# Batched product of x and y: loads of groups 4 to 11 issued from ScalarE's DMA queue instead of SyncE's, two steps later

## The chip, the cores and the metric

The kernel runs on one core of a Trainium2 chip. The metric is device time in microseconds (us), the median of 10 runs.

## The reference

For each of 96 pairs of batch and head (8 x 12), a 512 x 64 matrix x is multiplied by the transpose of a 512 x 64 matrix y. Inputs and output are float32.

```python
"x": np.random.randn(8, 12, 512, 64).astype(np.float32)
"y": np.random.randn(8, 12, 512, 64).astype(np.float32)
return np.einsum('bhtc,bhsc->bhts', x, y).astype(np.float32)
```

The inputs are 25.17 MB together, the output 100.66 MB. All of it crosses between HBM and SBUF once: 125.83 MB.

## The kernel before, in words

**Tiling.** The 96 heads are cut into 12 groups of 8 (`NG` = 12, `G` = 8). One group's x is one 1 MB load, xs, of 128 partitions with 8 KB each; its y is another, ys. A group gives four results of 2 MB (`half` 0 and 1, `h` 0 and 1), each gathered in one output tile `ot` of 128 partitions with 16 KB each and written by one store. So there are 24 loads and 48 stores.

**Stages of one group.** `casts` (L72) turns each half of xs and ys into bf16 in twelve instructions, which for groups 1 to 11 are all on GpSimd (L136). `transposes` (L100) makes xT and yT on VectorE with two 32 x 32 block transposes per half. `result` (L114) multiplies: for each k of 0, 2, 4, 6 two matmuls fill a PSUM tile `pm` of 128 x 1024, which is copied to `ot`, on ScalarE for k = 0, 2 and 6 (L128), on VectorE for k = 4 (L126). Then SyncE issues the store (L129).

**What sets the order.** The whole program stands under `manual_schedule`: each engine carries out its instructions in the order in which the Python code emits them. The main loop (L154) emits the four results of group g and, between their k steps, the preparation of group g + 1 as a generator, `prepare` (L131), of 16 steps; each k of each result takes one step. Steps 0 and 1 emit the casts, 5 and 13 the transposes, and step 12, which falls at k = 0 of the fourth result, emits the load of three groups further on (`AHEAD` = 3, L139). An engine that waits for a semaphore holds up everything behind it in its own order.

**The loads.** Groups 0, 1 and 2 are loaded at the start (L144) and group 3 after the casts of group 0 (L152). Groups 4 to 11 are loaded at step 12. All of them are issued on SyncE, as are the stores, so that loads and stores stand in one queue in the order of issue: from group 4 on two loads, then four stores, then two loads. A load waits until the casts have read the buffers that it overwrites.

**Buffers.** xs and ys have three buffers each, `ot` has seven, `pm` four. The framework also gives each DMA one of eight semaphores, in turn; a DMA whose semaphore still belongs to an unfinished one waits for that.

Of the kernel before, what the change touches and what calls it, by code (L numbers as in the profile page):

```python
# [1 line left out]

# [4 lines left out]


@with_exitstack
def kernel(  # L10
    ctx: ExitStack,
    tc: tile.TileContext,
    x: bass.AP,
    y: bass.AP,
    out: bass.AP,
):

    nc = tc.nc
    B, H, T, C = x.shape
    _, _, S, _ = y.shape
    P = 128
    G = 8
    Q = P // G  # L30
    R = T // Q
    NG = B * H // G
    K = 8
    E = R // K
    D = 32
    AHEAD = 3
    fp32 = mybir.dt.float32
    bf16 = mybir.dt.bfloat16
    u32 = mybir.dt.uint32
    COPY = mybir.ActivationFunctionType.Copy  # L40
    assert C == 2 * D and S == T and R == D and Q * 2 == D

    xv = x.rearrange("b h t c -> (b h t c)").rearrange("(g p n) -> g p n", p=P, n=R * C)
    yv = y.rearrange("b h t c -> (b h t c)").rearrange("(g p n) -> g p n", p=P, n=R * C)
    ov = out.rearrange("b h t s -> (b h t s)").rearrange(
        "(o u h q n) -> o h q u n", u=2, h=2, q=Q * E, n=K * S
    )

    const = ctx.enter_context(tc.tile_pool(name="const", bufs=1))
    lpool = ctx.enter_context(tc.tile_pool(name="lpool", bufs=AHEAD))  # L50
    ybpool = ctx.enter_context(tc.tile_pool(name="ybpool", bufs=2))
    tpool = ctx.enter_context(tc.tile_pool(name="tpool", bufs=4))
    opool = ctx.enter_context(tc.tile_pool(name="opool", bufs=7))
    pmpool = ctx.enter_context(tc.tile_pool(name="pmpsum", bufs=4, space=bass.MemoryType.PSUM))

    loaded, made = {}, {}
    zeroed = [const.tile([P, K * E * D], u32, name=f"xb{half}") for half in range(2)]

    def load(g):
        xs = lpool.tile([P, R, C], fp32)  # L60
        ys = lpool.tile([P, R, C], fp32)
        nc.sync.dma_start(xs.rearrange("p r c -> p (r c)"), xv[g])  # L62
        nc.sync.dma_start(ys.rearrange("p r c -> p (r c)"), yv[g])  # L63
        loaded[g] = (xs, ys)

    def cast(engine, dst, src):
        if engine is nc.scalar:
            nc.scalar.activation(dst, src, COPY)  # L68
        else:
            engine.tensor_copy(dst, src)  # L70

    def casts(g, half, engines):  # L72

        xs, ys = loaded[g]
        xb = zeroed[half]
        xv2 = xb.bitcast(bf16).rearrange("p (k e c u) -> p k e c u", k=K, e=E, u=2)
        base = half * 64
        n = 0
        for ch in range(2):
            for u in range(2):  # L80
                lo = base + u * D
                src = xs[lo:lo + D, :, ch * D:(ch + 1) * D]
                cast(
                    engines[n % len(engines)],
                    xv2[(2 * ch + u) * D:(2 * ch + u + 1) * D, :, :, :, u],
                    src.rearrange("p (e k) c -> p k e c", k=K),
                )
                n += 1
        yb = ybpool.tile([P, R // 2 * D], u32)
        yv2 = yb.bitcast(bf16).rearrange("p (j c w) -> p j w c", j=R // 2, w=2)  # L90
        for ch in range(2):
            cast(
                engines[n % len(engines)],
                yv2[ch * 64:(ch + 1) * 64],
                ys[base:base + 64, :, ch * D:(ch + 1) * D].rearrange("p (j w) c -> p j w c", w=2),
            )
            n += 1
        return xb, yb

    def transposes(g, half, xb, yb):  # L100
        xT = tpool.tile([P, K * D * E], u32)
        nc.vector.transpose(  # L102
            xT.rearrange("p (k r e) -> p k e r", k=K, e=E),
            xb.rearrange("p (k e c) -> p k e c", k=K, e=E),
        )
        yT = tpool.tile([P, D * R // 2], u32)
        nc.vector.transpose(  # L107
            yT.rearrange("p (r j) -> p j r", r=D), yb.rearrange("p (j c) -> p j c", c=D)
        )
        made[g, half] = (  # L110
            xT.bitcast(bf16).rearrange("p (k h m) -> p k h m", k=K, h=2), yT.bitcast(bf16)
        )

    def result(g, half, h, steps):  # L114

        xT, yT = made[g, half]
        ot = opool.tile([P, K, S], fp32)
        for k in range(0, K, 2):
            next(steps, None)
            pm = pmpool.tile([P, 2, S], fp32)  # L120
            for two in range(2):
                nc.tensor.matmul(  # L122
                    pm[:, two, :], xT[:, k + two, h, :], yT[:, h * S:(h + 1) * S], start=True, stop=True
                )
            if k == 4:
                nc.vector.tensor_copy(ot[:, k:k + 2, :], pm)  # L126
            else:
                nc.scalar.activation(ot[:, k:k + 2, :], pm, COPY)  # L128
        nc.sync.dma_start(ov[2 * g + half, h], ot.rearrange("p r s -> p (r s)"))  # L129

    def prepare(g):  # L131

        b = {}
        for step in range(16):
            if step in (0, 1):
                b[step] = casts(g, step, [nc.gpsimd])  # L136
            if step in (5, 13):
                transposes(g, step // 8, *b[step // 8])
            if step == 12 and g + AHEAD < NG:  # L139
                load(g + AHEAD)  # L140
            yield

    with tc.manual_schedule():
        for g in range(AHEAD):  # L144
            load(g)
        nc.vector.memset(zeroed[0], 0.0)  # L146
        nc.gpsimd.memset(zeroed[1], 0.0)  # L147
        b0 = casts(0, 0, [nc.vector, nc.scalar, nc.gpsimd])
        transposes(0, 0, *b0)
        b1 = casts(0, 1, [nc.gpsimd, nc.scalar])  # L150
        transposes(0, 1, *b1)
        if AHEAD < NG:  # L152
            load(AHEAD)
        for g in range(NG):  # L154
            steps = prepare(g + 1) if g + 1 < NG else iter(())
            for half in range(2):
                for h in range(2):
                    result(g, half, h, steps)
            for _ in steps:
                pass  # L160


# [1 line left out]
_INS = ['x', 'y']  # L164
_OUTS = [((8, 12, 512, 512), 'float32')]


# [23 lines left out]
```

## Time and profile before

| | |
|---|---|
| median of 10 runs | 304.45 us (303.43 to 305.06) |
| the profiled execution, its own time | 305.01 us |
| its span | 303.1 us |
| busy: PE, DVE, ACT, POOL | 45%, 43%, 48%, 60% |
| DMA queue of SyncE (q1) | 98.2% of 16 engines' span |
| load, from issue to landing | 26.2 us (xs), 26.5 us (ys), median of 12 each |
| store, from issue to landing | 32.8 us, median of 48 |

The busy shares are of the span of the profiled execution. POOL is GpSimd, DVE is VectorE, ACT is ScalarE, PE is TensorE, and SP is SyncE, which only issues. A share of the DMA queue is the time that its packets took, summed, over 16 times the span. The span lies 1.9 us below the execution's own time.

### The profile page before, as it was taken

The page shows a single profiled execution, that of the slowest core. Times are in us where ns is not written, and L with a number is a line of the kernel's source. Part 1 is how long each engine was busy: PE and PEld are TensorE (multiplying, and loading weights), DVE is VectorE, ACT ScalarE, POOL GpSimd, SP SyncE. Part 2 cuts the span into 40 slices and gives each one's busy share as a digit, 9 for nine tenths or more (in the row PEclk, how much of TensorE's full clock was granted, in tenths as well). Part 3 has the DMA queues.
Part 4 walks back from the last instruction along what each step waited for, and adds up shares of the span by engine and source line. Part 5 has one row for each costly group of instructions (what it writes and reads, how often), then busy time and mean ns, then how long its engine had stood idle before and what let it go on. Part 6 is the DMA issues. An engine that isn't in the chain of part 4 may idle for free.

```text
span 303.1 us, 1551 instructions
## 1 busy us (share of the span) xinstructions
PE 135.3 (45%) x384; PEld 46.5 (15%) x384; DVE 130.8 (43%) x99; ACT 145.0 (48%) x150; POOL 182.1 (60%) x142
## 2 busy tenths in 40 slices
PE   0567766654632554445184264444527556430000
PEld 0112222221210111111021021111102212100000
DVE  3856666666670651544247065154334661310000
ACT  2996656585561553364256064347334655650000
POOL 3899999999999985682772955668379100000000
PEclk9995767798995687598559567758955968975555
DMA  7999999999999999999999999999999999999992
GB/s 291 427 385 437 418 431 435 428 418 429 429 418 438 428 422 428 435 422 422 433 428 412 433 430 432 415 441 415 419 441 423 443 415 441 419 441 423 437 428 106
DMA packets 10377, 125.93 MB, mean 415 GB/s; under 512 B 1152, under 2 KB 1152, under 8 KB 1152
## 3 DMA queue, kind: packets, MB, share of 16 engines
q1 hardware_dynamic: 10368, 125.83, 98.2%
q8 instruction: 3, 0.05, 0.1%
q14 instruction: 6, 0.05, 0.0%
HBM read 25.17 MB, written 100.66 MB: 415 GB/s over the span
## 4 chain that ended last, share of the span: by engine, by line
DMA 75%; POOL 10%; ACT 2%; issue 1%; DVE 0%; ACTq 0%; PE 0%; SPq 0%; POOLq 0%
DMA out_dram<-ot 62%; DMA ys<-in_y_dram 12%; POOL xb L70 6%; POOL yb L70 3%; ACT ot L128 2%; DVE ot L126 0%; PE pm L122 0%; ACTq L186 0%; SPq L62 0%; POOLq L70 0%; ACTq L128 0%; SPq L129 0%; DVE yT L107 0%; SPq L63 0%
## 5 line engine op out<-in xcount | busy, mean ns | idle before, releaser
L128 ACT ACTIVATE ot<-pm 128x1024 f32<-128x1024 f32 x144 | 137.0, 1028 | 120.5 <-DMA out_dram<-ot 99.8
L122 PE MATMUL pm<-yT,xT 128*128 128x512 bf16 x384 | 135.3, 507 | 132.5 <-ACT ot L128 98.6
L70 POOL CAST xb<-xs 32x1024 bf16<-32x1024 f32 x91 | 120.4, 1323 | 50.0 <-DMA xs<-in_x_dram 32.1
L126 DVE COPY ot<-pm 128x1024 f32<-128x1024 f32 x48 | 58.1, 1215 | 114.8 <-DMA out_dram<-ot 108.6
L122 PEld LDWEIGHTS <-xT 128*128 128x128 bf16 x384 | 46.5, 121 | 220.5 <-issue 195.5
L70 POOL CAST yb<-ys 64x1024 bf16<-64x1024 f32 x46 | 60.5, 1316 | 3.3 <-DMA ys<-in_y_dram 0.6
L102 DVE STREAM_TRANSPOSE xT<-xb 128x1024 uint32<-128x1024 uint32 x24 | 49.3, 2053 | 13.3 <-POOL xb L70 11.9
L107 DVE STREAM_TRANSPOSE yT<-yb 128x512 uint32<-128x512 uint32 x24 | 24.9, 1038 | 6.2 <-POOL yb L70 6.2
L70 DVE CAST xb<-xs 32x1024 bf16<-32x1024 f32 x2 | 2.5, 1237 | 3.7 <-DMA xs<-in_x_dram 3.7
L68 ACT ACTIVATE xb<-xs 32x1024 bf16<-32x1024 f32 x3 | 4.0, 1345 | 0.1
L68 ACT ACT_TABLE_LOAD x1 | 1.3, 1283 | 5.6 <-DMA xs<-in_x_dram 5.6
L68 ACT ACTIVATE yb<-ys 64x1024 bf16<-64x1024 f32 x2 | 2.7, 1350 | 0.0
L146 DVE MEMSET xb<- 128x1024 uint32 x1 | 0.9, 912 | 1.0 <-PEq L175 1.0
L147 POOL MEMSET xb<- 128x1024 uint32 x1 | 1.0, 951 | 0.3 <-POOLq L175 0.3
L175 POOL MEMSET const-float32-0.0<- 128x1 f32 x1 | 0.1, 97 | 0.2 <-issue 0.2
L175 POOL MEMSET const-float32-1.0<- 128x1 f32 x1 | 0.1, 98 | 0.0
L175 POOL MEMSET const-bfloat16-1.0<- 128x1 bf16 x1 | 0.1, 98 | 0.0
L175 POOL MEMSET const-uint8-127<- 128x1 uint8 x1 | 0.1, 98 | 0.0
## 6 DMA issues: line engine op xcount, KB each, us to landing
out_dram<-ot SPq DMA_DIRECT2D x48, 2048.0 KB, 32.8
xs<-in_x_dram SPq DMA_DIRECT2D x12, 1024.0 KB, 26.2
ys<-in_y_dram SPq DMA_DIRECT2D x12, 1024.0 KB, 26.5
```

Source lines behind the costliest of these rows:

```text
L68: nc.scalar.activation(dst, src, COPY)
L70: engine.tensor_copy(dst, src)
L102: nc.vector.transpose(xT.rearrange("p (k r e) -> p k e r", k=K, e=E), xb.rearrange("p (k e c) -> p k e c", k=K, e=E),)
L107: nc.vector.transpose(yT.rearrange("p (r j) -> p j r", r=D), yb.rearrange("p (j c) -> p j c", c=D))
L122: nc.tensor.matmul(pm[:, two, :], xT[:, k + two, h, :], yT[:, h * S:(h + 1) * S], start=True, stop=True)
L126: nc.vector.tensor_copy(ot[:, k:k + 2, :], pm)
L128: nc.scalar.activation(ot[:, k:k + 2, :], pm, COPY)
L146: nc.vector.memset(zeroed[0], 0.0)
L147: nc.gpsimd.memset(zeroed[1], 0.0)
L175: nc = _bacc.Bacc("TRN2", target_bir_lowering=False, num_devices=1)
```

## The change

`load` gets the queue as an argument. The loads of groups 0 to 3 stay on SyncE. Those of groups 4 to 11 are emitted at step 14 in place of 12, and are issued by ScalarE. Step 14 falls at k = 4 of the fourth result. In ScalarE's order the two issues stand between the copies of k = 2 and of k = 6 of that result, and nothing else moves on ScalarE, VectorE, GpSimd or TensorE. SyncE is left with the first eight loads and then 48 stores in a row.

```diff
-    def load(g):
+    def load(g, queue):
...
-        nc.sync.dma_start(xs.rearrange("p r c -> p (r c)"), xv[g])
-        nc.sync.dma_start(ys.rearrange("p r c -> p (r c)"), yv[g])
+        queue.dma_start(xs.rearrange("p r c -> p (r c)"), xv[g])
+        queue.dma_start(ys.rearrange("p r c -> p (r c)"), yv[g])
...
-            if step == 12 and g + AHEAD < NG:
-                load(g + AHEAD)
+            if step == 14 and g + AHEAD < NG:
+                load(g + AHEAD, nc.scalar)
...
-            load(g)
+            load(g, nc.sync)
...
-            load(AHEAD)
+            load(AHEAD, nc.sync)
```

## Prediction

> **What bounds the kernel now.** I read the slices of the page first, then its queues, its chain and its DMA issues.
>
> ```profile
> DMA  7999999999999999999999999999999999999992
> GB/s 291 427 385 437 418 431 435 428 418 429 429 418 438 428 422 428 435 422 422 433 428 412 433 430 432 415 441 415 419 441 423 443 415 441 419 441 423 437 428 106
> DMA packets 10377, 125.93 MB, mean 415 GB/s; under 512 B 1152, under 2 KB 1152, under 8 KB 1152
> ...
> q1 hardware_dynamic: 10368, 125.83, 98.2%
> ...
> DMA 75%; POOL 10%; ACT 2%; issue 1%; DVE 0%; ACTq 0%; PE 0%; SPq 0%; POOLq 0%
> ...
> out_dram<-ot SPq DMA_DIRECT2D x48, 2048.0 KB, 32.8
> xs<-in_x_dram SPq DMA_DIRECT2D x12, 1024.0 KB, 26.2
> ```
>
> From the second slice to the last but one the 16 DMA engines are never short of work, and the chain is 75% DMA. A store lands 32.8 us after its issue, although 2.10 MB take only 4.9 us at 430 GB/s: some six transfers are queued ahead of it. The waits say the same from the other side: the evicting engines wait for output buffers to be written out.
>
> ```profile
> DVE ot L126 <- DMA out_dram<-ot: 108.6, 31, 9.5
> ACT ot L128 <- DMA out_dram<-ot: 99.8, 33, 7.9
> ...
> POOL xb L70 <- DMA xs<-in_x_dram: 32.1, 6, 6.3
> ```
>
> So the time is what the DMA engines need for 125.83 MB, and any microsecond that they gain or lose counts in full. How much is lost already? Stretches with and without loads, from the table of windows (last two columns: DMA share, GB/s):
>
> ```profile
> 94.00:143.00 49.00, 22.69 (x64) 7.72 (x64) 21.12 (x16) 22.84 (x24) 34.82 (x27) 0.72 1.01 428
> 143.00:192.00 49.00, 22.53 (x61) 7.49 (x61) 21.15 (x16) 22.75 (x24) 30.41 (x25) 0.66 1.01 426
> 192.00:219.00 27.00, 12.52 (x37) 4.26 (x36) 10.51 (x8) 11.52 (x13) 17.32 (x14) 0.79 1.00 425
> 225.00:290.00 65.00, 26.26 (x72) 8.70 (x71) 20.31 (x16) 28.13 (x30) 8.24 (x7) 0.68 1.01 431
> ```
>
> Stores alone (the last row) run at 431, loads and stores mixed at 425 to 428. A group moves 10.49 MB, which is 24.33 us at 431 and 24.56 at 427: about 0.2 us lost per group.
>
> The trace's packet records say where. The 72 transfers have 144 packets each: 128 with data and 16 of 4 bytes that close them, so each engine gets 8 data packets of each transfer. A store packet (16 KB) is recorded with 611 ns, a load packet (8 KB) with 309; on one engine the next starts some 4 ns before the last ends, so their pitch is 607 and 306 ns. Only one place is regularly longer: the last load packet of a pair of loads, the one with a store behind it. Over the eight later pairs the excess per engine is 0.08, 0.15, 0.11, 0.12, 0.24, 0.28, 0.15 and 0.20 us, mean 0.16. The first load packet behind a store shows none. I call this cost, of going from a load to a store on one engine, a turn. As a check: an engine starts at 1.87 us, its first packet comes 0.73 us late, and 384 x 0.607 + 192 x 0.306 + 72 x 0.006 = 292.3, so without turns it would end at 294.9. Ten of the 16 engines end at 296.3 to 296.6, mean 296.4: 1.55 us late, of which the first turn, at 23 us, is 0.63 (10.2 us of excess over 16 engines). The other eight turns have the remaining 0.92, or **0.115 us each**, somewhat less than the records' excess. The other six engines end up to 5.5 us later, at 301.9; behind instruction and table fetches (9 packets on q8 and q14) they fall back, and the slowest sets the end.
>
> **What the Trainium skill says.** "DMA: Bandwidth & Descriptors", section "Queues, rings and completion order": SP and ACT each have a ring of their own on each of the same 16 engines, and an engine goes round-robin between the rings that have work, a packet at a time; a packet there may be some 9 to 17 descriptors. The trace before has one busy ring, but shows the granularity: five of the six 8 KB fetches on q14 came between two store packets. They took 309 to 311 ns, and the store packet behind them took 722, 964, 881, 716 and 960 ns in place of 611. That is a turn between two rings, of 0.11 to 0.35 us, mean 0.24. The same page, "Issuing engines are not separate DMA queues", says that issuing from several engines saves only issue time; SP isn't short of that here. Against me stands its section "Latency and other measured facts": copies of 128 x 16 KB tiles on the sync and scalar queues at 214 GB/s per direction, called full. That is 428 both ways, no less than here, if those queues alternated as these will; the page doesn't say how transfers were spread over them.
>
> **The change part by part.**
>
> *Issues leave SP.* Sixteen issues of 0.33 us: nothing, because SP waits most of the time.
>
> ```profile
> SPq L129 <- DMA out_dram<-ot: 59.6, 14, 4.5
> SPq L63 <- DMA out_dram<-ot: 23.4, 6, 4.5
> SPq L129 <- DMA xs<-in_x_dram: 15.4, 7, 2.5
> ```
>
> *Issues go to ACT, at step 14.* Sixteen times about 0.33 us, 5.3 us on an engine that is idle for 158 us. Behind them on ACT stand the copies of k = 6 of the fourth result and then the next result; SP's store waits for these. If the load must wait for GpSimd's casts, this lasts no longer than SP's waits for POOL do now (at most 2.4 us at once). In steady state GpSimd is done earlier: at 161.1 us, where ACT would reach step 14 at about 166. Cover: a queue of some 28 us (32.8 - 4.9), and 9.5 us at the least (shortest landing, early). Cost 0. Without that cover it would be up to 8 x 2.7 = 22 us (2.4 of wait and 0.33 of issue).
>
> *Semaphores.* In the changed order, the store of a group's first result waits on the semaphore of the y load that ACT issued in the fourth result just before. That takes 16 alternating packets, about 17 us, in which two of some six queued stores pass. Four are left, and nothing runs dry: cost 0.
>
> *Two rings in place of one.* This is the term that counts. Bytes and packets stay. Of each group, 16 load packets per engine now sit in ACT's ring beside a ring of stores that is never empty, so they alternate: load, store, load, store. A group has 16 turns instead of 1, and there are 8 such groups: 8 x 16 = 128 in place of 8, so 120 more. What a turn costs in steady alternation the trace doesn't show. Lower bound: nothing, and then the 8 x 0.115 = 0.9 us of today's turns may go too (the skill's copies). Upper bound: 0.24 us, the fetches' mean, so 128 x 0.24 - 0.9 = 29.8 us. I take 0.115, what undisturbed engines really lose per turn in one ring: 120 x 0.115 = **13.8 us**.
>
> Sum: 305.01 + 13.8 = 318.8 us for an execution like the profiled one, which lies 0.56 above the median; against the median, 304.45 + 13.8 = **318.3 us**. The late engines stay late, since their fetches remain. Their 5.5 us are the most that better balance could bring; I see no reason why it should.
>
> **The rivals.**
> - *The turn is hidden* (the other side, not slower). With a ring of its own, a load packet's data could be read while a store packet is being written, and a turn costs nothing. Place: the 8 turns that there are now; price: 0.9 us less, 303.5 us. It decides if a turn costs under 0.9 / 128 = 7 ns. For it: the skill's copies, and no cost from store to load now. Against it: every store behind a fetch was longer. If turns cost 4 to 12 ns, the time is within 0.2%.
> - *Coarser or cheaper alternation.* If an engine drains a transfer's 8 packets before it changes rings, a group has two turns, after x and after y: 8 x 0.115 = 0.9 more, 305.4 us. The skill's 9 to 17 descriptors would fit. Against it: the fetches that came between single packets. Turns of 15 to 60 ns, partly hidden, give 305.5 to 311 us.
> - *ACT's wait empties the queue.* Up to 22 us, 326 us; it needs a store queue under 2.7 us deep, and it is at least 9.5.
>
> **How the numbers follow.** About 0.2% is what a measurement of this kernel can tell from no change. Turns of 0.08 to 0.25 us with packetwise alternation: 50%, own range 314 to 335 us. Coarser or partly hidden: 22%. Hidden: 26%, of which 16% faster by over 0.2% and 10% within it. ACT's wait: 2%. Slower thus 74%. The range goes from the hidden case with room for noise, 303.0, to 332; above it lie turns over 0.22 us (some 6%), below it a gain of over 0.5% (some 9%).
>
> **What would show it.** A second hardware queue with 16 x 144 = 2304 packets. With 24 KB per 0.607 + 0.306 + 0.115 us on 16 engines, about 382 GB/s where both rings are busy, and about 400 over a whole group (26.2 us in place of 24.5); 431 for the stores at the end, as before. ACT's loads landing in about 17 us rather than 26, GpSimd no longer waiting for xs, waits for `ot` longer, DMA still never idle. I am wrong if mixed stretches hold 425 or more, if loads pass in runs of 8 packets, or if the DMA share falls, which would put the cost in an empty queue and not in turns.

## The result and the profile after

The changed kernel takes 305.62 us (median of 9 runs, 305.02 to 306.2), the kernel before in the same measurement 304.62 us (32 runs). The ratio is 1.0039, 95% interval 1.0026 to 1.0052: slower by some 1.0 us. The forecast was 318.3. The profiled execution of the changed kernel took 305.17 us, with a span of 303.3 us.

From the page of the changed kernel: the slices, the queues, the chain, and the DMA issues (count, KB each, us to landing).

```profile
DMA  7999999999999999999999999999999999999991
GB/s 292 424 381 442 415 443 422 425 430 429 432 425 432 425 434 419 439 428 419 430 430 420 426 442 407 428 433 437 426 434 430 432 428 430 434 425 437 424 432 69
...
q1 hardware_dynamic: 8064, 109.06, 84.8%
q10 hardware_dynamic: 2304, 16.78, 13.1%
...
DMA 67%; POOL 17%; ACT 2%; issue 2%; DVE 0%; ACTq 0%; PE 0%; SPq 0%; POOLq 0%; DVEq 0%
...
out_dram<-ot SPq DMA_DIRECT2D x48, 2048.0 KB, 31.2
xs<-in_x_dram ACTq DMA_DIRECT2D x8, 1024.0 KB, 12.0
ys<-in_y_dram ACTq DMA_DIRECT2D x8, 1024.0 KB, 18.9
```

The second queue is q10, with the 2304 packets foretold. The DMA engines are as full as before; x and y land 12 and 19 us after their issue instead of 26. The waits of the changed kernel (us in total, times, longest):

```profile
DVE ot L126 <- DMA out_dram<-ot: 112.6, 34, 5.9
ACT ot L128 <- DMA out_dram<-ot: 98.7, 35, 4.5
...
ACT ot L128 <- POOL yb L70: 7.9, 3, 3.9
...
POOL xb L70 <- DMA xs<-in_x_dram: 4.0, 1, 4.0
```

GpSimd no longer waits for xs (32.1 us before). ScalarE waits three times for GpSimd's casts, 3.9 us at most, behind its load. No slice of the DMA line shows a gap for it. The windows of before, taken again on the changed kernel (last two columns: DMA share, GB/s):

```profile
94.00:143.00 49.00, 27.77 (x64) 8.90 (x63) 20.90 (x16) 23.06 (x24) 34.13 (x27) 0.53 1.01 429
143.00:192.00 49.00, 24.20 (x60) 8.10 (x59) 18.75 (x16) 21.78 (x23) 30.84 (x24) 0.67 1.01 427
192.00:219.00 27.00, 15.54 (x42) 5.32 (x40) 12.85 (x10) 12.70 (x14) 16.80 (x13) 0.75 1.01 431
...
225.00:290.00 65.00, 25.86 (x72) 8.56 (x71) 20.29 (x16) 28.00 (x30) 9.04 (x7) 0.66 1.01 430
```

Mixed stretches run at 427 to 431 GB/s, where 382 to 400 were forecast, and before at 425 to 428: no loss beside that of before. (In the third window the loads are done by 203 us.) And do the queues alternate? From 112 to 120 us of the changed kernel, by queue (packets, MB, share):

```profile
q1 hardware_dynamic: 158, 2.29, 67.7%
q10 hardware_dynamic: 155, 1.14, 33.7%
```

Both move about ten packets per engine in these 8 us. Runs of eight packets would give equal counts too, as eight stores and eight loads take 7.3 us, so the order has to be read from the packet records. Followed engine by engine, 1532 of the 1759 unbroken runs of q10's load packets are a single packet, 210 are two and none is longer than six: the queues do alternate, nearly always packet by packet. But there is no turn in it: the 2048 load packets of q10 have 309.5 ns on average (309 undisturbed). A store packet behind a load packet has a median of 611 ns, as if undisturbed, and on average 1.8 to 3.5 ns more in four profiles of the changed kernel.

**Where the time is.** What ends the program is not the mass of the transfers but the last engine. The end in windows, first of the kernel before, then of the changed one; 1.00 in the column before the last is 16 engines busy, so 0.06 is one:

```profile
295.00:297.00 2.00, 0.00 (x0) 0.00 (x0) 0.00 (x0) 0.00 (x0) 0.00 (x0) 0.50 0.75 320
297.00:299.00 2.00, 0.00 (x0) 0.00 (x0) 0.00 (x0) 0.00 (x0) 0.00 (x0) 0.50 0.29 123
299.00:301.00 2.00, 0.00 (x0) 0.00 (x0) 0.00 (x0) 0.00 (x0) 0.00 (x0) 0.50 0.17 74
301.00:303.00 2.00, 0.00 (x0) 0.00 (x0) 0.00 (x0) 0.00 (x0) 0.00 (x0) 0.50 0.04 16
```

```profile
295.00:297.00 2.00, 0.00 (x0) 0.00 (x0) 0.00 (x0) 0.00 (x0) 0.00 (x0) 0.50 0.62 262
297.00:299.00 2.00, 0.00 (x0) 0.00 (x0) 0.00 (x0) 0.00 (x0) 0.00 (x0) 0.50 0.23 98
299.00:301.00 2.00, 0.00 (x0) 0.00 (x0) 0.00 (x0) 0.00 (x0) 0.00 (x0) 0.50 0.13 57
301.00:303.00 2.00, 0.00 (x0) 0.00 (x0) 0.00 (x0) 0.00 (x0) 0.00 (x0) 0.50 0.02 8
```

In the changed kernel fewer engines are still at work in each of these windows: the mass of them ends earlier. Only the last one does not, with 302.12 us against 301.93 in these two profiles, and the span ends 1.2 us behind it in both.

### The profile page after: what moved, and what is told of

Same layout as the page of the kernel before. It is cut to its first block, busy times and chain, and to the rows that moved or that the text cites. A ratio compares the mean times of both kernels' runs of the same rounds, so it can differ in the third digit from the quotient of the medians.

```text
span 303.3 us, 1544 instructions
## 1 busy us (share of the span) xinstructions
PE 144.0 (47%) x384; PEld 48.6 (16%) x384; DVE 130.3 (43%) x99; ACT 145.7 (48%) x150; POOL 182.1 (60%) x142
## 3 DMA queue, kind: packets, MB, share of 16 engines
q10 hardware_dynamic: 2304, 16.78, 13.1%
## 4 chain that ended last, share of the span: by engine, by line
DMA 67%; POOL 17%; ACT 2%; issue 2%; DVE 0%; ACTq 0%; PE 0%; SPq 0%; POOLq 0%; DVEq 0%
DMA out_dram<-ot 65%; POOL xb L70 11%; POOL yb L70 6%; DMA ys<-in_y_dram 2%; ACT ot L128 2%; DVE ot L126 0%; ACTq L186 0%; PE pm L122 0%; SPq L62 0%; POOLq L70 0%; ACTq L128 0%; DVEq L126 0%; SPq L129 0%; DVE yT L107 0%
## 5 line engine op out<-in xcount | busy, mean ns | idle before, releaser
L122 PE MATMUL pm<-yT,xT 128*128 128x512 bf16 x384 | 144.0, 536 | 124.0 <-ACT ot L128 71.7
L122 PEld LDWEIGHTS <-xT 128*128 128x128 bf16 x384 | 48.6, 127 | 218.5 <-issue 196.9
```

The lines of the kernel that those rows point to most:

```text
L122: nc.tensor.matmul(pm[:, two, :], xT[:, k + two, h, :], yT[:, h * S:(h + 1) * S], start=True, stop=True)
```

## The experiments

Theory A was formed from these traces: alternation is free; a cost arises only where loads begin beside running stores (or, in one queue, where a store follows a load), and it is the latest engine that pays most and sets the time. Rivals: B, the prediction's cost per change; C, the two steps or ScalarE's issue do it. "Ends" below are the last closing packet of each of the 16 engines, from the packet records. A "stall" is a packet recorded at least 60 ns longer than its undisturbed 309 or 611 ns; a record tells no engine, so stalls of one engine are found by following packets, each beginning where the last one ended. By this count the kernel before has, after 25 us, 84 stalls on load packets and 11 on stores, 22.4 us over all engines; the changed kernel has 1 and 51, 13.2 us. So the stalls moved from loads to stores and became less, by some 0.6 us per engine.

### The queue alone, and the steps alone

Queue12: ScalarE's queue, but at step 12. Sp14: SyncE's queue, at step 14.

```diff
# queue12, against the changed kernel
-            if step == 14 and g + AHEAD < NG:
+            if step == 12 and g + AHEAD < NG:
```

```diff
# sp14, against the kernel before
-            if step == 12 and g + AHEAD < NG:
+            if step == 14 and g + AHEAD < NG:
```

> The changed kernel with its loads on ScalarE's queue, but at step 12 as before: the queue alone. Theory A (the queue does it: the engines alternate for free, and a load's arrival beside running stores costs only at the first store behind it; the slowest engine pays most): the same as the changed kernel, 305.6 us, 1.003 to 1.005 of before. Theory C (the two steps do it, because ScalarE's issue or the later load holds up a store): 304.5 us, 1.000 of before.

> The kernel before with its loads two steps later, still on SyncE's queue: the steps alone. Theory A: 304.5 us, 1.000 of before, because the order of transfers in SyncE's queue is the same. Theory C: 305.5 us, 1.003.

Queue12: 305.33 us, ratio to before 1.0021 (1.0006 to 1.0036). Sp14: 304.72 us, 0.9998 (0.9985 to 1.0011). The steps alone do nothing and the queue alone is slower. ScalarE's wait is not the reason either: in queue12 ScalarE waits 17.1 us for the casts, 8.3 at once, against 7.9 and 3.9 in the changed kernel, and queue12 is not the slower of the two. So C falls. The two steps may add something on ScalarE's queue; the intervals of queue12 and of the changed kernel overlap.

### Twice as many changes from load to store

Split: each load of groups 4 to 11 in two halves of 4 KB per partition.

```diff
-        queue.dma_start(xs.rearrange("p r c -> p (r c)"), xv[g])
-        queue.dma_start(ys.rearrange("p r c -> p (r c)"), yv[g])
+        parts = 1 if queue is nc.sync else 2
+        n = R * C // parts
+        for tile_, view in ((xs, xv), (ys, yv)):
+            flat = tile_.rearrange("p r c -> p (r c)")
+            for i in range(parts):
+                queue.dma_start(flat[:, i * n:(i + 1) * n], view[g][:, i * n:(i + 1) * n])
```

> The changed kernel with each load of groups 4 to 11 in two halves of 4 KB per partition: 32 load packets per group and engine instead of 16, so 256 changes from load to store per engine instead of 128, and ScalarE's queue holds loads for nearly the whole of each group. Theory A (alternation is free, only a beginning costs): no more than the changed kernel, 304.5 to 306 us. Theory B, the prediction's (each change costs some 0.1 us): 128 more changes are at least 10 us more, 315 us or above.

Measured: 303.9 us, 0.9976 (0.9968 to 0.9984), faster than both kernels. The queues and the issues on ScalarE in its profile:

```profile
q1 hardware_dynamic: 8064, 109.06, 84.8%
q10 hardware_dynamic: 4608, 16.78, 13.6%
...
xs<-in_x_dram ACTq DMA_DIRECT2D x16, 512.0 KB, 12.9
ys<-in_y_dram ACTq DMA_DIRECT2D x16, 512.0 KB, 23.7
```

4608 packets on q10, and no time lost: B falls by more than 10 us. Loads pass without a pause of over 1 us from 64.1 to 212.3 us. There are 9 stalls on stores (2.4 us in all) after 25 us, against 51 (12.7 us) in the changed kernel, and 14 on loads (2.1 us) against 1.

### More places where a store follows a load, in one queue

Sp_two_turns: all on SyncE, y moved behind the first store of the next group. (`load`, left out here, is told the queue and which of x and y to load.)

```diff
-            if step == 12 and g + AHEAD < NG:
-                load(g + AHEAD)
+            if step == 12 and g + AHEAD < NG:
+                load(g + AHEAD, nc.sync, "x")
+            if step == 4 and AHEAD < g - 1 + AHEAD < NG:
+                load(g - 1 + AHEAD, nc.sync, "y")
```

> The kernel before, all on SyncE's queue, with the y load of each group moved behind the first store of the next group: 16 places per engine where a store follows a load instead of 8. If each place costs what the ten engines that end together lose (0.085 us), 8 more are 0.7 us, 305.2 us, ratio 1.002. If the time is set by the latest engine, which loses 0.5 to 0.7 us at each such place, 8 more are 4 to 5 us, 308.5 to 309.5 us, ratio 1.013 to 1.017, with the ten engines still ending within 1 us of where they did.

Measured: 309.78 us, 1.0158 (1.0134 to 1.0182). The end of its profile, in windows as above:

```profile
295.00:297.00 2.00, 0.00 (x0) 0.00 (x0) 0.00 (x0) 0.00 (x0) 0.00 (x0) 0.50 0.63 270
297.00:299.00 2.00, 0.00 (x0) 0.00 (x0) 0.00 (x0) 0.00 (x0) 0.00 (x0) 0.50 0.19 82
299.00:301.00 2.00, 0.00 (x0) 0.00 (x0) 0.00 (x0) 0.00 (x0) 0.00 (x0) 0.50 0.19 82
301.00:303.00 2.00, 0.00 (x0) 0.00 (x0) 0.00 (x0) 0.00 (x0) 0.00 (x0) 0.50 0.13 57
303.00:305.00 2.00, 0.00 (x0) 0.00 (x0) 0.00 (x0) 0.00 (x0) 0.00 (x0) 0.50 0.08 33
305.00:307.00 2.00, 0.00 (x0) 0.00 (x0) 0.00 (x0) 0.00 (x0) 0.00 (x0) 0.50 0.06 25
```

Between 297 and 301 us three engines of 16 are busy (0.19), at the end one. The first ten ends are at 295.8 to 296.4 us, no later than before; the last is at 306.95 instead of 301.93. The whole 5.2 us lie in a few late engines, 0.65 us per added place: that the latest engine pays most, a part of A, is seen here, in one profile.

### Fewer places and beginnings: two groups at a time

Both kernels load two groups together in every second group: sp_pairs on SyncE from the kernel before, act_pairs on ScalarE from the changed one.

```diff
-    lpool = ctx.enter_context(tc.tile_pool(name="lpool", bufs=AHEAD))
+    lpool = ctx.enter_context(tc.tile_pool(name="lpool", bufs=AHEAD + 1))
...
-    tpool = ctx.enter_context(tc.tile_pool(name="tpool", bufs=4))
+    tpool = ctx.enter_context(tc.tile_pool(name="tpool", bufs=3))
...
# act_pairs; sp_pairs has the same at step 12, on SyncE
-            if step == 14 and g + AHEAD < NG:
+            if step == 14 and g % 2 and g + AHEAD < NG:
                 load(g + AHEAD, nc.scalar)
+                load(g + AHEAD + 1, nc.scalar)
```

> The kernel before, all on SyncE's queue, with the loads of two groups issued together in every second group (four input buffers, three for the transposed tiles): 4 places where a store follows a load instead of 8. If the latest engine loses 0.65 us at each place, as 8 more of them cost 5.2 us, 4 fewer give 2.6 us back: 301.9 us, ratio 0.991. If the places count only what the engines that end together lose (0.085 us), 304.2 us, ratio 0.999.

> The changed kernel with the loads of two groups issued together in every second group (four input buffers, three for the transposed tiles): the loads begin beside running stores 4 times instead of 8. If the beginnings are what the changed kernel pays, 1.7 us for 8 by its distance to the split one, 4 fewer give 0.85 us back: 304.7 us, ratio 1.000 to 1.001. If it pays for something else, it stays at 305.6 us, 1.003.

Sp_pairs: 304.14 us, 0.9981 (0.9972 to 0.999). It gained 0.5 us, not 2.6: a place does not cost the latest engine a constant sum. Act_pairs: 302.67 us, 0.9948 (0.9933 to 0.9963), the fastest of all, where 304.7 was expected. The end of act_pairs:

```profile
295.00:297.00 2.00, 0.00 (x0) 0.00 (x0) 0.00 (x0) 0.00 (x0) 0.00 (x0) 0.50 0.52 221
297.00:299.00 2.00, 0.00 (x0) 0.00 (x0) 0.00 (x0) 0.00 (x0) 0.00 (x0) 0.50 0.12 49
299.00:301.00 2.00, 0.00 (x0) 0.00 (x0) 0.00 (x0) 0.00 (x0) 0.00 (x0) 0.50 0.00 0
```

Four engines end after 297 us, two of them within 0.4 us, and none after 299.13. There are 24 stalls on stores after 25 us, 5.6 us in all.

### Is it the pairs or the buffers? And do the two gains add?

Act_buf4 is the changed kernel with the buffers of act_pairs only. Pairs_split is act_pairs with the halves of split.

```diff
# act_buf4, against the changed kernel
-    lpool = ctx.enter_context(tc.tile_pool(name="lpool", bufs=AHEAD))
+    lpool = ctx.enter_context(tc.tile_pool(name="lpool", bufs=AHEAD + 1))
...
-    tpool = ctx.enter_context(tc.tile_pool(name="tpool", bufs=4))
+    tpool = ctx.enter_context(tc.tile_pool(name="tpool", bufs=3))
```

> The changed kernel with the buffers of the paired one (four input buffers, three for the transposed tiles), but loads issued group by group as in the changed kernel. If the paired kernel gained by its issue in pairs, this stays at 305.6 us, ratio 1.003. If it gained by the buffers, because a load waits for nothing, it falls to 302.7 us, ratio 0.995.

> The paired kernel with each load in two halves of 4 KB per partition. Both of its edits made the changed kernel faster (split 1.7 us, pairs 2.9 us). If both do it by fewer pauses of the loads, together they give no more than the better one, 302.5 to 304 us. If they act on different things, they add: 301 to 302 us.

Act_buf4: 304.93 us, 1.0016 (0.9997 to 1.0035). Of the 2.9 us by which act_pairs beats the changed kernel, the buffers give 0.7 by the medians, and perhaps nothing, as the intervals of act_buf4 and of the changed kernel overlap; the rest is the issue in pairs. Pairs_split: 304.38 us, 0.9989 (0.9974 to 1.0004). The gains don't add, and the halves undo most of what the pairs gave: they brought 41 stalls of load packets (11.5 us), and the first ten engines end at 297.2 to 298.3 us, over 1 us later than in the changed kernel.

### More beginnings, and shorter first packets

Two_entries issues y eight steps after x, so that loads should begin 16 times. In its packet records they begin 13 times (after a pause of over 1 us), against 8 in the changed kernel. X_split halves x only.

```diff
# two_entries, against the changed kernel
-            if step == 14 and g + AHEAD < NG:
-                load(g + AHEAD, nc.scalar)
+            if step == 14 and g + AHEAD < NG:
+                load(g + AHEAD, nc.scalar, "x")
+            if step == 6 and AHEAD < g - 1 + AHEAD < NG:
+                load(g - 1 + AHEAD, nc.scalar, "y")
```

```diff
# x_split, against split
-        parts = 1 if queue is nc.sync else 2
-        n = R * C // parts
         for tile_, view in ((xs, xv), (ys, yv)):
+            parts = 2 if queue is nc.scalar and tile_ is xs else 1
+            n = R * C // parts
```

> The changed kernel with the y load of each group issued eight steps after the x load, at step 6 of the next group: the loads begin beside running stores 16 times instead of 8. If beginnings cost 1.7 us for 8, it is 307.3 us, ratio 1.009. If they cost nothing and something else makes the difference, it stays at 305.6 us, 1.003.

> The changed kernel with only the x loads in two halves of 4 KB per partition, y whole: 24 load packets per group and engine, so that loads still pause in each group and begin 8 times, but the first packets are of 4 KB. If the split kernel was faster because its loads hardly ever pause, this stays near the changed kernel, 305.2 to 305.8 us. If the smaller packet was the reason, it goes to 304.4 us or less.

Two_entries: 305.87 us, 1.0038 (1.0021 to 1.0054), like the changed kernel: more beginnings don't cost more, and A's count of beginnings falls. X_split: 305.95 us, 1.0039 (1.0025 to 1.0053), just above the 305.2 to 305.8 expected if it is the missing pause and not the small packet that helped split.

### Four profiles of each kernel

Each kernel was profiled three more times, unchanged.

> The changed kernel once more, for a second profile. If the time is that of the latest of the 16 DMA engines, the mean engine ends near 297.4 us again, and the span follows the latest one, some 1.2 us behind it, wherever that ends.

> The kernel before once more, for a second profile. The mean engine ends near 297.8 us again, 0.4 us later than that of the changed kernel, and the span ends some 1.2 us behind the latest engine.

> A third profile of the changed kernel. Of the changed kernel and of the kernel before there will be four profiles each. If the 1.0 us that the change costs lie in the latest engine alone, the first ten engines end about 0.4 us earlier in the changed kernel, as in the first two pairs of profiles, and the latest one, on average, 1.0 us later.

> A third profile of the kernel before, for the same count: its first ten engines end near 296.6 us, its latest near 302 us.

> A fourth profile of the changed kernel, for the same count: its first ten engines end near 296.2 us, its latest between 302 and 303 us.

> A fourth profile of the kernel before, for the same count: its first ten engines end near 296.6 us, its latest near 302 us.

Ends in us, mean of the four profiles:

| | before | changed |
|---|---|---|
| first ten engines | 296.63 | 296.12 |
| all 16 | 297.96 | 297.24 |
| last but one | 301.43 | 299.76 |
| last | 302.04 | 302.36 |
| the executions' own times | 305.10 | 305.43 |

The change makes the mean end 0.7 us earlier and the last engine but one 1.7 us earlier; each profile of the changed kernel lies below every one of before in both. The last engine sets the time and gains nothing. That it is 0.3 us later on average rests on one profile: it ends at 301.95 to 302.19 us in three of the changed kernel and at 303.19 in the fourth, against 301.89 to 302.25 before. So the profiles show why the gain of the mass is lost. Where the 1.0 us of the medians come from they do not show; the four profiled executions of before happen to lie above their median of 304.6, and of the 1.0 us only 0.3 is seen here.

Following the last engine of the changed kernel back through its packets gives the same story in three of the four profiles: at 60.9 to 61.4 us it carries a 16 KB fetch on q8 of 0.96 us. From then on it is out of step with the others, and it stalls where loads begin and where y follows x. In the first profile this is 0.24 us at 111.9, 0.30 at 119.5, 0.37 at 136.2, 0.55 at 137.2 and 0.31 at 145.1; the loads began at 111.7 and 136.6 there, and y at about 119 and 144. In these three profiles there are eleven such stalls up to 196.5 us, 4.0 to 4.3 us in all. In the first, where the last engine ends 6.1 us behind one that had neither fetch nor stall, the fetch and the packet behind it make up 1.4.

A fetch is not needed for it. In the remaining profile (after_3) the last engine carries none; its first long stalls come at 63 to 66 us, where loads begin, and it loses 6.7 us in 21 stalls, while the engine with the q8 fetch at 61.7 us ends at 299.79. In the first profile an engine without any fetch ends at 299.94 after 19 stalls.

In act_pairs the engine with the fetch at 61.0 us has four such stalls, 1.3 us in all, and is last but one. The last engine there is late in another way: about 200 of its stores are longer by some 12 ns each, 2.3 us in all. Each of the four profiles of the changed kernel has such an engine too, which ends at 299.1 to 299.5 us. That lateness and stalls go together is seen; why an engine out of step stalls there is not, nor why one engine's stores are longer, and no kernel without the fetches was tried.

## Why the prediction was wrong, point by point

- **What bounds the kernel**: right in that the DMA engines are never idle. Incomplete in that the time is the latest engine's. The prediction saw the 5.5 us of lag and set it aside ("The late engines stay late, since their fetches remain"). The lag is not a constant of the fetches: one edit took the last end from 301.93 to 306.95 us with the first ten ends no later, another to 299.13, and engines without a fetch are late too. (What the prediction calls table fetches, the profile lists as instruction, on q8 and q14 alike.)
- **The step that failed**: "Two rings in place of one", 120 more turns of 0.115 us, 13.8 us. The alternation came nearly as foretold, with some 110 changes from load to store per engine instead of 128. Their price was wrong: 0.002 to 0.004 us on average and not 0.115, with a median of nothing. By this the 128 turns come to less than 0.5 us. The prediction had named the sign of being wrong, 425 GB/s or more in mixed stretches; they held 427 to 431. Two readings led there. The longer last load packet of a pair was taken as a price of every change. In the records it is one of the last load packets in a queue behind which stores wait, and it is all but gone where queues alternate (84 stalls on loads before, 1 after). And the longer stores behind the q14 fetches, 0.11 to 0.35 us, were taken as a change between two busy queues; they follow a queue that comes in for one packet, and don't recur where two queues alternate for long. Why a fetch costs more than a load packet is not shown. The 428 GB/s that the prediction held as evidence against itself, twice the 214 GB/s per direction that the Trainium skill gives for copies between HBM tensors ("DMA: Bandwidth & Descriptors", section "Latency and other measured facts"), agree with the 427 to 431 measured here.
- **Issues off SP, issues on ACT, semaphores**: no cost of theirs is seen, as foretold. ACT waited 7.9 us for casts in three places, 3.9 at once and longer than the 2.4 taken, and SyncE waited 72.6 us for loads whose semaphores its stores needed, 13.5 at once; the queue of stores covered both, with a DMA share of 1.00 or more in all windows from 45 to 290 us. Sp14 shows that on SyncE the two steps alone are free.
- **The rival "hidden"**: its price held, nothing per change, and of the 16 ends, taken in order, the first 15 came earlier on average over four profiles (0.5 us for the first ten, 0.9 foretold). That a load's read runs beside a store's write, as it supposed, no run shows. Its time did not come, for the sixteenth engine.
- **The rival "coarser"**: its 305.4 us is near the measured 305.6 by chance. Its mechanism, runs of 8 packets, did not happen: the longest run of load packets in the first profile is six, and 87% are a single packet. So what an engine took from one queue before it changed was nearly always one data packet, and the 9 to 17 descriptors that the prediction held to fit are not seen in the records.
- **What stays open**: where most of the 1.0 us arises, as the last engine's end differs clearly in one profile of four only, and why an engine out of step stalls where loads begin in a second queue. It isn't the number of beginnings (two_entries). Fewer stalls went with a better time in split and act_pairs, but not in step: split has fewer stalls on stores than act_pairs and is 1.2 us slower.

## What to carry to other kernels

With a queue that is always full, don't price a change of direction from a single event (a fetch, the end of a block of loads) times the number of changes; whether it recurs when two queues alternate is a question for a run. Look at the last microseconds by engine share: if a few of 16 engines work alone there, the time is a matter of lag. Here the placement of the loads among the stores moved it by several microseconds (299.13 to 306.95 us for the last engine) while the first ten ended at 295.9 to 296.4 us on average in the same profiles. Here loads on a second queue, issued for two groups at a time, gave 0.5% over the kernel before; the same loads group by group lost 0.4%.

## What the runs showed of the hardware that was not expected

- Two queues that both had work alternated nearly always a data packet at a time, 16 KB against 8 KB (1532 of the 1759 runs of loads in the first profile), with next to no price per change: 309.5 ns per load packet on average over 2048 packets, against 309, and 1.8 to 3.5 ns more on average for a store behind a load.
- A 16 KB instruction fetch took 0.92 to 0.97 us of one DMA engine, and the store behind it was mostly 0.35 to 0.41 us longer.
- In one queue, an engine that was late lost far more at each place where a store follows a load (0.65 us per place in sp_two_turns) than an engine in step (0.085 us: 0.68 us of excess over eight places, mean of the first ten ends of before). So its lag grew. It is no constant sum: four places fewer gained 0.5 us in sp_pairs.
- In each of four profiles of the changed kernel and in act_pairs, one engine lost 2.0 to 2.6 us outside of stalls, by some 200 stores that were each about 12 ns longer.
